# First MLP product of seven column groups by seven block products in place of eight, with the sums of weight blocks on VectorE

## The chip, the core and the metric

The kernel runs on one core of a Trainium2 chip. The core has a matrix engine (TensorE, rows PE for its matmuls and PEld for the loads of its stationary operand), VectorE (DVE), ScalarE (ACT), GpSimd (POOL, unused here) and a queue that issues transfers (SP). They run beside each other and wait for one another by semaphores. The working memory is SBUF; TensorE writes into the banks of PSUM, of which there are eight of 128 x 512 float32. The metric is the device time of one execution in microseconds.

## What is computed

One layer of a hybrid decoder for 256 tokens of width 2048 behind 16 learned tokens: token mixing (gated linear attention and pooling), then a multilayer perceptron (MLP) with 8192 hidden columns, each part added to the residual `h`, and a last norm. All is float32. What matters here:

```python
h = h + mixed @ w_out
z = rmsnorm(h, norm2_w) @ mlp_w1                  # [256, 2048] @ [2048, 8192]
h = h + jnp.square(jax.nn.relu(z)) @ mlp_w2       # [256, 8192] @ [8192, 2048]
return rmsnorm(h, final_norm_w)
```

## The kernel before

**Numbers in two parts.** TensorE runs in a float32 form of reduced precision (`F32R`), so each operand is held as a rounded part `hi` and a rest `lo`, and each product of tiles is three matmuls: hi·hi, hi·lo, lo·hi. The weights come as raw float32 chunks of 128 x 2048 (1 MB), one transfer each (`raw_chunk`, L92, pool `rawp` with 3 buffers), in the order of use. `halves` (L99) splits a chunk into two halves of 128 x 1024: `split` (L74) rounds on ACT (L75, `hi`) and subtracts on DVE (L76, `lo`). The pools `hip` and `lop` have 4 buffers each, so four halves can lie ready or in use.

**The MLP.** The hidden columns are cut into 8 groups of 1024. `mlp1(g)` (L671) makes a group's hidden values: two strips of 512 columns, each from four chunks; `as_chunk` (L208) does one chunk with 24 matmuls of 128 x 512, four k-tiles times the two token tiles times three parts (L217 to L219), into two PSUM banks. The stationary operand is the normed input `u2_hi`, `u2_lo`; the weights stream. At the end of a strip ACT and DVE take relu and square out of PSUM (L683, L685), with the squared 1/rms as the scale, and a deferred step (`back`) turns the result with four transposes per token tile (`turn4`, L635) and splits it (`evac_hl`, L495 to L497) into `z_hi`, `z_lo`. `mlp2(g)` (L697) multiplies them with the group's rows of the second matrix: four strips of two chunks, added to `h` by `add_h` (L627). The loop runs `mlp1(g)`, then `mlp2(g-1)`. The last group's second product stands by itself (L714 to L786), one token tile after the other, with the last norm; its weight `fw` is loaded and scaled early (`load_fw`, `scale_fw`).

**Order.** Deferred steps stand in the list `side`; `run_side` issues one behind each half of a chunk. The framework then puts each engine's instructions into a fixed queue, by the order of the code and by when operands and buffers are expected to be free; each engine works its queue from front to back. `tile_pool(bufs=n)` gives n buffers; a new tile waits until the users of an old one are done.

Of the kernel before, what the change touches and what calls it, by code (L numbers as in the profile page):

```python
# [7 lines left out]
F32 = mybir.dt.float32  # L8
# [3 lines left out]
ALU = mybir.AluOpType  # L12
# [18 lines left out]
# columns of the constants that depend on shapes alone  # L31
# [5 lines left out]
def hybrid_gla_pool_kernel(  # L37
# [35 lines left out]
    # ---------------------------------------------------------------- weights  # L73
# [34 lines left out]
    # -------------------------------------------------------------- constants  # L108
# [14 lines left out]
    # u = rmsnorm(h) without 1/rms, transposed: [channel, token]  # L123
# [21 lines left out]
    # ------------------------------------------------------------- 1 / rms  # L145
# [43 lines left out]
    # --------------------------------------- matrix products, three exact parts  # L189
# [33 lines left out]
    # ================================================================ phase 1  # L223
    # keys: four row blocks at once, in pieces that grow, as the first loads arrive
# [76 lines left out]
    # low-rank gate input, transposed; rows 0..15 and 32..47 add up  # L301
# [14 lines left out]
    # log gates over natural tokens (the factor 1/16 sits in the triangles)  # L316
# [27 lines left out]
    # ke: meta tokens to their end, tile 0 to its end, the first chunk of each tile to its end  # L344
# [43 lines left out]
    # values  # L388
# [24 lines left out]
    # queries  # L413
# [85 lines left out]
    # output gate  # L499
# [38 lines left out]
    # multi-scale pooling  # L538
# [83 lines left out]
    u2_hi = big.tile([P, KD, S], F32R, tag="u_hi", name="u2_hi")  # L622
    u2_lo = big.tile([P, KD, S], F32R, tag="u_lo", name="u2_lo")
# [14 lines left out]
    def make_u2(s, t):  # L638
        ps = turn4(h[:, t, s * 512 : (s + 1) * 512])
        ts = slice(t * P, (t + 1) * P)  # L640
        for j in range(4):
            k = 4 * s + j
            pj = ps[:, j * P : (j + 1) * P]
            act.activation(u2_hi[:, k, ts], pj, AF.Copy, scale=n2[:, k : k + 1])
            dve.scalar_tensor_tensor(
                out=u2_lo[:, k, ts], in0=pj, scalar=n2[:, k : k + 1],
                in1=u2_hi[:, k, ts].bitcast(F32), op0=ALU.mult, op1=ALU.subtract,
            )
# [18 lines left out]
    dve.tensor_tensor(out=rs2, in0=rs2, in1=rs2, op=ALU.mult)  # L667
# [3 lines left out]
    def mlp1(g):  # L671
        nonlocal ci
        z_hi = mp.tile([P, 8, S], F32R, tag="m", name="z_hi")
        z_lo = mp.tile([P, 8, S], F32R, tag="m", name="z_lo")
        rz[g] = (z_hi, z_lo)
        for s in range(2):
            ps = [acc(), acc()]
            for c in range(4):
                as_chunk(ps, ci, u2_hi, u2_lo, 0, 4, 4 * c, c == 0, c == 3)
                ci += 1  # L680
            for t in range(NT):
                r = zt.tile([P, 512], F32, tag="r", name="r")
                act.activation(r, ps[t], AF.Relu, scale=rs2[:, t : t + 1])  # L683
                q = zt.tile([P, 512], F32, tag="q", name="q")
                dve.scalar_tensor_tensor(  # L685
                    out=q, in0=ps[t], scalar=0.0, in1=r, op0=ALU.max, op1=ALU.mult
                )


                def back(s=s, t=t, q=q):  # L690
                    pv = turn4(q).rearrange("p (j c) -> p j c", c=P)
                    ts = slice(t * P, (t + 1) * P)
                    evac_hl(z_hi[:, 4 * s : 4 * s + 4, ts], z_lo[:, 4 * s : 4 * s + 4, ts], pv)

                side.append(back)

    def mlp2(g):  # L697
        nonlocal ci
        z_hi, z_lo = rz.pop(g)
        for s in range(4):  # L700
            ps = [acc(), acc()]
            for c in range(2):
                as_chunk(ps, ci, z_hi, z_lo, 0, 4, 4 * c, c == 0, c == 1)
                ci += 1
            for t in range(NT):
                add_h(ps[t], t, s * 512, (s + 1) * 512)

    mlp1(0)
    side += [load_fw, idle, idle, idle, scale_fw]
    for g in range(1, GROUPS):  # L710
        mlp1(g)
        mlp2(g - 1)
    # ======================================= last group: one token tile after the other
    z_hi, z_lo = rz.pop(GROUPS - 1)  # L714
    e_hi = big.tile([P, KD, S], F32R, tag="u_hi", name="e_hi").rearrange("p k c -> p (k c)")
    e_lo = big.tile([P, KD, S], F32R, tag="u_lo", name="e_lo").rearrange("p k c -> p (k c)")

    def finish(t, w, ps, n):
        # 1/rms out of the sum so far and of the last w columns, still in ps
# [69 lines left out]
def _weights(np, w_in, w_out, w1, w2):  # L789
    """All weights as one run of chunks [128, 2048], in the order in which they are used."""  # L790
    def ws(a):  # [2048, n*256] -> n strips of two chunks, each 8 k-tiles of 256 columns
        n = a.shape[1] // 256
        b = a.reshape(2, 8, P, n, 256).transpose(3, 0, 2, 1, 4)
        return b.reshape(n * 2, P, 2048)

    def st(a):  # [512*c, n*512] -> [n, c] chunks, each 4 k-tiles of 512 columns
# [19 lines left out]
    for g in range(1, GROUPS):  # L816
        m1(g)
# [59 lines left out]
```

## Time and profile before

| | |
|---|---|
| time, median of 3 runs | 1049.33 us (1048.45 to 1050.74) |
| span of the profiled execution | 1046.9 us |
| TensorE matmul busy | 1035.2 us (99%), 5237 matmuls |
| weight load busy | 877.2 us (84%) |
| DVE busy | 605.9 us (58%) |
| ACT busy | 480.6 us (46%) |
| transfers | 197.15 MB, 188 GB/s over the span |

The span is the time from the first to the last instruction; no time of the profiled execution as a whole is given, and the median of the runs is 2.4 us above the span. Matmuls are pipelined and the end of each is modelled, so a matmul's listed time (0.39 us) is longer than the distance to the next one; the distance is the price. Likewise on DVE and ACT a listed time is that of one instruction from its start to its end.

### The profile page before, as it was taken

To read this page: it belongs to the slowest core of one execution; us is meant where nothing else is said; L and a number is where in the kernel's file an instruction comes from. 1 tells how busy PE (TensorE), PEld (TensorE's weight loads), DVE (VectorE), ACT (ScalarE), POOL (GpSimd) and SP (SyncE) were. 2 spreads that over 40 slices of the span, in tenths; PEclk is the share of its full clock that TensorE was granted. 3 is DMA by queue.
4 is the path that set the end of the run, shared out by engine and by line. 5 is a ranking of instruction groups with operands and counts; after the bars stand their busy time and mean duration, and the time that the engine had idled before them with its cause. 6 is when DMAs were issued, how large, how long until landed. Compare 5 with 4: busy or idle time off the path is not lost.

```text
span 1046.9 us, 12935 instructions
## 1 busy us (share of the span) xinstructions
PE 1035.2 (99%) x5237; PEld 877.2 (84%) x5237; DVE 605.9 (58%) x773; ACT 480.6 (46%) x630; POOL 0.2 (0%) x4
## 2 busy tenths in 40 slices
PE   8999999999999999999999999999999999999996
PEld 7989878998888888888888888888888888888885
DVE  7555544876666555555555555565555555555574
ACT  6537544444555444434434433443443344344351
POOL 0000000000000000000000000000000000000000
PEclk9999999999999999999999999999999999999998
DMA  9663434447554545555555555555555555545542
GB/s 348 241 239 137 161 124 159 146 155 288 186 190 172 201 173 189 198 184 182 201 189 179 196 194 184 185 200 186 182 197 191 185 188 199 185 178 201 188 174 81
DMA packets 29820, 197.15 MB, mean 188 GB/s; under 512 B 3456, under 2 KB 3968, under 8 KB 6704
## 3 DMA queue, kind: packets, MB, share of 16 engines
q1 hardware_dynamic: 29760, 196.32, 52.9%
q8 instruction: 41, 0.67, 0.3%
q14 instruction: 19, 0.16, 0.0%
HBM read 194.21 MB, written 2.10 MB: 188 GB/s over the span
## 4 chain that ended last, share of the span: by engine, by line
PE 98%; DMA 1%; SPq 0%; DVE 0%; ACT 0%; issue 0%; ACTq 0%
PE acc L217 25%; PE acc L219 25%; PE acc L218 25%; PE acc L202 4%; PE acc L203 4%; PE acc L204 4%; PE gp L635 2%; PE acc L777 1%; PE acc L776 1%; PE acc L778 1%; DMA raw<-in_wts 1%; PE acc L256 1%; PE acc L258 1%; PE acc L257 1%; PE gp L472 0%; PE gp L473 0%
## 5 line engine op out<-in xcount | busy, mean ns | idle before, releaser
L76 DVE TENSOR_TENSOR lo<-raw,hi 128x1024 fp32r<-128x1024 f32 (+1 forms) x356 | 425.8, 1200 | 373.6 <-ACT hi L75 373.3
L75 ACT CAST hi<-raw 128x1024 fp32r<-128x1024 f32 (+1 forms) x356 | 366.1, 1033 | 484.2 <-PE acc L219 409.4
L217 PE MATMUL acc<-hi,u_hi 128*128 128x512 f32 x576 | 228.5, 397 | 0.0
L219 PE MATMUL acc<-hi,u_lo 128*128 128x512 f32 x576 | 224.8, 390 | 0.0
L218 PE MATMUL acc<-lo,u_hi 128*128 128x512 f32 x576 | 224.5, 390 | 0.0
L217 PE MATMUL acc<-hi,z_hi 128*128 128x512 f32 x448 | 175.7, 392 | 0.0
L219 PE MATMUL acc<-hi,z_lo 128*128 128x512 f32 x448 | 174.5, 389 | 0.0
L218 PE MATMUL acc<-lo,z_hi 128*128 128x512 f32 x448 | 174.4, 389 | 0.0
L219 PEld LDWEIGHTS acc<-hi,u_lo 128*128 128x128 f32 x576 | 108.1, 188 | 23.0
L217 PEld LDWEIGHTS acc<-hi,u_hi 128*128 128x128 f32 x576 | 108.2, 188 | 22.0
L218 PEld LDWEIGHTS acc<-lo,u_hi 128*128 128x128 f32 x576 | 108.3, 188 | 21.7
L219 PEld LDWEIGHTS acc<-hi,z_lo 128*128 128x128 f32 x448 | 84.1, 188 | 17.7
L217 PEld LDWEIGHTS acc<-hi,z_hi 128*128 128x128 f32 x448 | 84.1, 188 | 17.1
L218 PEld LDWEIGHTS acc<-lo,z_hi 128*128 128x128 f32 x448 | 84.2, 188 | 17.0
L202 PE MATMUL acc<-u_hi,hi 128*128 128x272 f32 (+4 forms) x320 | 92.7, 290 | 0.0
L203 PE MATMUL acc<-u_lo,hi 128*128 128x272 f32 (+4 forms) x320 | 91.4, 286 | 0.0
L204 PE MATMUL acc<-u_hi,lo 128*128 128x272 f32 (+4 forms) x320 | 91.2, 285 | 0.0
L202 PEld LDWEIGHTS acc<-u_hi,hi 128*128 128x128 f32 x320 | 60.3, 189 | 1.0 <-issue 0.8
L203 PEld LDWEIGHTS acc<-u_lo,hi 128*128 128x128 f32 x320 | 60.2, 188 | 0.1
L204 PEld LDWEIGHTS acc<-u_hi,lo 128*128 128x128 f32 x320 | 60.1, 188 | 0.0
L627 DVE TENSOR_TENSOR h<-acc,h 128x512 f32<-128x512 f32 (+1 forms) x71 | 45.6, 679 | 5.2 <-PE acc L778 5.2
L683 ACT ACTIVATE r<-acc,rs 128x512 f32<-128x512 f32 x32 | 21.9, 690 | 15.7 <-PE acc L219 15.7
(189 smaller groups left out, 841.6 us busy)
## 6 DMA issues: line engine op xcount, KB each, us to landing
raw<-in_wts SPq DMA_DIRECT2D x175, 1024.0 KB, 4.8
xn<-in_x SPq DMA_DIRECT2D x2, 1024.0 KB, 11.8
h<-in_x SPq DMA_DIRECT2D x2, 1024.0 KB, 6.7
out<-h SPq DMA_DIRECT2D x8, 256.0 KB, 2.9
xTs<-in_xT SPq DMA_DIRECT2D x3, 546.0 KB, 9.7
pw<-in_pool_w SPq DMA_DIRECT2D x4, 256.0 KB, 5.1
fw<-in_rows SPq DMA_DIRECT2D x1, 1024.0 KB, 7.7
raw<-in_wts SPq DMA_DIRECT2D x2, 256.0 KB, 3.5
```

What stands on the lines that cost most here:

```text
L75: act.copy(out=hi, in_=raw)
L76: dve.tensor_tensor(out=lo, in0=raw, in1=hi.bitcast(F32), op=ALU.subtract)
L202: pe.matmul(o, hi[:, cs], u_hi[:, k, lo_t:L], start=k == 0, stop=False)
L203: pe.matmul(o, hi[:, cs], u_lo[:, k, lo_t:L], start=False, stop=False)
L204: pe.matmul(o, lo[:, cs], u_hi[:, k, lo_t:L], start=False, stop=k == KD - 1)
L217: pe.matmul(ps[t], a_hi[:, k, ts], hi[:, cs], start=st, stop=False)
L218: pe.matmul(ps[t], a_hi[:, k, ts], lo[:, cs], start=False, stop=False)
L219: pe.matmul(ps[t], a_lo[:, k, ts], hi[:, cs], start=False, stop=sp)
L256: pe.matmul(o, hi[:, cs], u_hi[:, k, :], start=k == 0, stop=False)
L627: dve.tensor_tensor(out=hs, in0=p, in1=hs, op=ALU.add)
L635: pe.transpose(ps[:, j * P : (j + 1) * P], src[:, j * P : (j + 1) * P], ident)
L683: act.activation(r, ps[t], AF.Relu, scale=rs2[:, t : t + 1])
```

## The change

Groups 1 to 7 no longer call `mlp1`. Their hidden values are a product of [256 x 2048] and [2048 x 1024], seen as 2 x 2 blocks: token tiles times halves of the inner dimension, and these halves times two strips of 512 columns. `group(g)` makes the four blocks of the result from seven block products (`product`, of 128 x 1024 and 1024 x 512) and sums. The seven left operands are made once, in `prepare` (blocks, and sums and differences of blocks, of the input normed with 1/rms), during group 0, which keeps the direct way. The right operands are sums of raw weight blocks, made in place on DVE for each group (`add_raw`, eight additions of 128 x 2048) and split after that like any chunk. The products accumulate in three PSUM banks; `keep` copies three intermediate sums out, and `hidden` adds them where needed and takes relu and square. The eight chunks of the second product of the group before (`half(0)` to `half(7)`) stand between the seven products. The same bytes of weights are loaded, in another order. Pools change: `rawp` 4 buffers, `xy` (4 buffers of 8 KB per partition: first the input's `u2`, then the weight blocks `xs` and `zs`, last the tail's `e`), `zt` 2, and for the MLP 3 + 2 + 3 PSUM banks in place of 4 + 4. `fw` is loaded and scaled behind group 7.

```diff
-    big = ctx.enter_context(tc.tile_pool(name="big", bufs=1))
     mp = ctx.enter_context(tc.tile_pool(name="mp", bufs=4))
-    rawp = ctx.enter_context(tc.tile_pool(name="rawp", bufs=3))
+    rawp = ctx.enter_context(tc.tile_pool(name="rawp", bufs=4))
     hip = ctx.enter_context(tc.tile_pool(name="hip", bufs=4))
     lop = ctx.enter_context(tc.tile_pool(name="lop", bufs=4))
-    accp = ctx.enter_context(tc.tile_pool(name="accp", bufs=4, space=PSUM))
-    gpp = ctx.enter_context(tc.tile_pool(name="gpp", bufs=4, space=PSUM))
-    gt = ctx.enter_context(tc.tile_pool(name="gt", bufs=4))
+    banks = ctx.enter_context(ExitStack())
+    accp = banks.enter_context(tc.tile_pool(name="accp", bufs=4, space=PSUM))
+    gpp = banks.enter_context(tc.tile_pool(name="gpp", bufs=4, space=PSUM))
     gstack = ctx.enter_context(ExitStack())
+    big = gstack.enter_context(tc.tile_pool(name="big", bufs=1))
+    gt = gstack.enter_context(tc.tile_pool(name="gt", bufs=4))
     gq = gstack.enter_context(tc.tile_pool(name="gq", bufs=1))
...
+            gstack.close()
+            xy = ctx.enter_context(tc.tile_pool(name="xy", bufs=4))
+            lp = ctx.enter_context(tc.tile_pool(name="lp", bufs=1))
+            zt = ctx.enter_context(tc.tile_pool(name="zt", bufs=2))
+            gt = gstack.enter_context(tc.tile_pool(name="gt2", bufs=4))
...
-    u2_hi = big.tile([P, KD, S], F32R, tag="u_hi", name="u2_hi")
-    u2_lo = big.tile([P, KD, S], F32R, tag="u_lo", name="u2_lo")
+    u2 = [[xy.tile([P, 8, S], F32R, tag="xy", name="u2") for _ in range(2)] for _ in range(2)]
...
+    while side:
+        side.pop(0)()
+    gstack.close()
+    asp = ctx.enter_context(tc.tile_pool(name="asp", bufs=1))
...
+    def norm_a(kh):
+        a = mp.tile([P, 8, S], F32, tag="m", name="a")
+        full.append(a)
+        u_h, u_l = (u.bitcast(F32) for u in u2[kh])
+        dve.tensor_tensor(out=a, in0=u_h, in1=u_l, op=ALU.add)
+        dve.tensor_tensor(out=a, in0=a, in1=rb2.unsqueeze(1).to_broadcast([P, 8, S]), op=ALU.mult)
...
+    def operand(i, t, kh, sign=1.0):
+        a = blk(t, kh)
+        hi, lo = (asp.tile([P, 8, P], F32R, name=f"{n}{i}") for n in ("ah", "al"))
+        if sign > 0:
+            act.copy(out=hi, in_=a)
+            dve.tensor_tensor(out=lo, in0=a, in1=hi.bitcast(F32), op=ALU.subtract)
+        else:
+            act.activation(hi, a, AF.Copy, scale=-1.0)
+            dve.scalar_tensor_tensor(
+                out=lo, in0=a, scalar=-1.0, in1=hi.bitcast(F32), op0=ALU.mult, op1=ALU.subtract
+            )
+        ops_a[i] = (hi, lo)
...
+        def s5():
+            operand(4, 1, 1)
+            combine((1, 1), (1, 1), (1, 0), ALU.subtract)
+            operand(5, 1, 1)
+        def s7():
+            combine((1, 0), (0, 0), (1, 0), ALU.subtract)
+            operand(7, 1, 0)
+        def s6():
+            combine((0, 0), (0, 0), (1, 1), ALU.add)
+            operand(6, 0, 0, -1.0)
+        def s3():
+            combine((0, 1), (0, 0), (0, 1), ALU.subtract)
+            operand(3, 0, 1)
...
+        return [
+            rms2_rows, lambda: norm_a(0), lambda: operand(1, 0, 0), lambda: norm_a(1),
+            lambda: operand(2, 0, 1), s5, s7, s6, s3,
...
+    banks.close()
+    accp = ctx.enter_context(tc.tile_pool(name="pair", bufs=3, space=PSUM))
+    gpp = ctx.enter_context(tc.tile_pool(name="turn", bufs=2, space=PSUM))
+    sump = ctx.enter_context(tc.tile_pool(name="sum", bufs=1, space=PSUM))
+    def xy_load(c):
+        raw = xy.tile([P, 2048], F32, tag="xy", name="blk")
+        nc.sync.dma_start(out=raw, in_=wts[c])
+        return raw
...
+    def product(i, ps, raws, start):
+        a_hi, a_lo = ops_a[i]
+        for c in range(2):
+            for hf, (hi, lo) in enumerate(halves(raws[c])):
+                for j in range(2):
+                    k = c * 4 + hf * 2 + j
+                    cs = slice(j * 512, (j + 1) * 512)
+                    kw = dict(skip_group_check=True)
+                    pe.matmul(ps, a_hi[:, k], hi[:, cs], start=start and k == 0, stop=False, **kw)
+                    pe.matmul(ps, a_hi[:, k], lo[:, cs], start=False, stop=False, **kw)
+                    pe.matmul(ps, a_lo[:, k], hi[:, cs], start=False, stop=k == 7, **kw)
+            run_side()
...
+    def add_raw(dst, src):
+        dve.tensor_tensor(out=dst, in0=dst, in1=src, op=ALU.add)
+    def keep(ps, name):
+        x = zt.tile([P, 512], F32, tag=name, name=name, bufs=1)
+        act.copy(out=x, in_=ps)
+        return x
+    def hidden(g, s, t, ps, x, sign):
+        q = zt.tile([P, 512], F32, tag="q", name="q")
+        if x is None:
+            r = ps
+        else:
+            r = zt.tile([P, 512], F32, tag="r", name="r")
+            dve.tensor_tensor(out=r, in0=ps, in1=x, op=ALU.add)
+        act.activation(q, r, AF.Relu, scale=sign)
+        act.activation(q, q, AF.Square)
+        side.append(z_back(g, s, t, q))
...
+        def half(j):
+            if j % 2 == 0:
+                pair[:] = [acc(), acc()]
+            as_chunk(pair, base + 8 + j, z_hi, z_lo, 0, 4, 4 * (j % 2), j % 2 == 0, j % 2 == 1)
+            if j % 2:
+                for t in range(NT):
+                    add_h(pair[t], t, j // 2 * 512, (j // 2 + 1) * 512)
+        b_a, b_d, b_b = (sump.tile([P, 512], F32, tag=n, name=n) for n in ("sa", "sd", "sb"))
+        xs = [xy_load(base), xy_load(base + 1)]
+        zs = [xy_load(base + 2), xy_load(base + 3)]
+        product(1, b_a, xs, True)
+        x1 = keep(b_a, "x1")
+        add_raw(xs[0], zs[0])
+        half(0)
+        ys = [raw_chunk(base + 4), raw_chunk(base + 5)]
+        add_raw(xs[1], zs[1])
+        product(5, b_d, xs, True)
+        x5 = keep(b_d, "x5")
+        add_raw(xs[0], ys[0])
+        half(1)
+        add_raw(xs[1], ys[1])
+        product(3, b_d, ys, False)
+        half(2)
+        add_raw(zs[0], ys[0])
+        half(3)
+        add_raw(zs[1], ys[1])
+        product(6, b_a, xs, False)
+        x2 = keep(b_a, "x2")
+        hidden(g, 1, 0, b_d, x2, -1.0)
+        vs = [raw_chunk(base + 6), raw_chunk(base + 7)]
+        add_raw(xs[0], vs[0])
+        half(4)
+        add_raw(xs[1], vs[1])
+        product(7, b_a, zs, False)
+        hidden(g, 1, 1, b_a, x5, -1.0)
+        half(5)
+        product(4, b_a, xs, False)
+        hidden(g, 0, 1, b_a, None, 1.0)
+        half(6)
+        product(2, b_b, vs, True)
+        hidden(g, 0, 0, b_b, x1, 1.0)
+        half(7)
...
+    e = [[xy.tile([P, 2048], F32R, tag="xy", name="e") for _ in range(2)] for _ in range(2)]
+    fw = mp.tile([P, D], F32, tag="m", name="fw")
+    nc.sync.dma_start(out=fw, in_=rows[:, 768 : 768 + D].partition_broadcast(P))
+    dve.tensor_scalar(out=fw, in0=fw, scalar1=-1.0 / 8192.0, scalar2=None, op0=ALU.mult)
...
-        m1(g)
+        for kh, n in ((0, 0), (0, 1), (1, 1), (1, 0)):
+            parts.append(a[2 * g + n, 2 * kh : 2 * kh + 2])
```

## Rows read from the trace of the kernel before

**Rows 1.** The page: busy time by engine; the span in 40 slices.

```profile
PE 1035.2 (99%) x5237; PEld 877.2 (84%) x5237; DVE 605.9 (58%) x773; ACT 480.6 (46%) x630; POOL 0.2 (0%) x4
...
PE   8999999999999999999999999999999999999996
...
DVE  7555544876666555555555555565555555555574
...
PEclk9999999999999999999999999999999999999998
```

**Rows 2.** The chain by engine; then matmuls' waits (line, releaser: us, times, longest).

```profile
PE 98%; DMA 1%; SPq 0%; DVE 0%; ACT 0%; issue 0%; ACTq 0%
...
PE gp L119 <- DVE warm L116: 1.5, 1, 1.5
PE acc L256 <- ACT hi L75: 1.3, 2, 0.7
PE acc L258 <- DVE lo L76: 0.2, 1, 0.2
```

**Rows 3.** Stretches: length, busy us by engine, granted clock, DMA share, GB/s.

```profile
350.50:396.00 45.50, 45.50 (x211) 37.66 (x210) 24.79 (x25) 21.30 (x24) 0.00 (x0) 1.00 0.52 185
484.98:573.95 88.97, 88.97 (x402) 73.65 (x401) 49.13 (x49) 38.19 (x40) 0.00 (x0) 1.00 0.54 189
573.95:662.92 88.97, 88.97 (x403) 73.66 (x401) 49.15 (x49) 38.18 (x40) 0.00 (x0) 1.00 0.53 189
```

**Rows 4.** Timeline of PE, a strip: 19th matmul behind the first; chain, one bank alone.

```profile
477.33 0.39 PE L217 MATMUL acc<-hi,u_hi 128*128 128x512 f32 x1
...
481.41 0.39 PE L217 MATMUL acc<-hi,u_hi 128*128 128x512 f32 x1
...
1030.37 0.23 PE acc L776
...
1031.73 0.23 PE acc L776
```

**Rows 5.** The chain, start us, us: the four transposes of one token tile.

```profile
484.98 0.44 PE gp L635 x4
```

**Rows 6.** DVE and ACT by shape, 485 to 930 us: count, busy, mean ns, idle before.

```profile
L76 DVE TENSOR_TENSOR lo<-raw,hi 128x1024 fp32r<-128x1024 f32 x161 | 197.2, 1225 | 194.9 <-ACT hi L75 194.9
L627 DVE TENSOR_TENSOR h<-acc,h 128x512 f32<-128x512 f32 x40 | 25.6, 682 | 0.0
...
L75 ACT CAST hi<-raw 128x1024 fp32r<-128x1024 f32 x161 | 169.6, 1054 | 245.2 <-PE acc L219 245.2
L683 ACT ACTIVATE r<-acc,rs 128x512 f32<-128x512 f32 x20 | 13.7, 690 | 9.9 <-PE acc L219 9.9
```

**Rows 7.** DVE by shape, whole span: the longest two-operand forms, and `fw`'s scaling.

```profile
L335 DVE SCALAR_TENSOR_TENSOR lg<-g,lg 128x1536 f32<-128x1536 f32 x1 | 1.8, 1759 | 3.3 <-ACT lg L334 3.3
...
L615 DVE TENSOR_SCALAR fw<-fw 128x2048 f32<-128x2048 f32 x1 | 1.2, 1222 | 0.0
```

**Rows 8.** Timeline of DVE: instructions without a gap (merged, xcount), and what follows.

```profile
13.74 2.50 DVE L76 TENSOR_TENSOR lo<-raw,hi 128x512 fp32r<-128x512 f32 x4 [0.84 <-ACT hi L75]
16.16 1.73 DVE L135 SCALAR_TENSOR_TENSOR u_lo<-xTs,u_hi 128x272 fp32r<-128x272 f32 x4
...
32.54 3.49 DVE L76 TENSOR_TENSOR lo<-raw,hi 128x1024 fp32r<-128x1024 f32 x3
```

**Rows 9.** ACT by shape, whole span: the last load of its function table.

```profile
L482 ACT ACT_TABLE_LOAD x1 | 1.3, 1283 | 0.0
```

**Rows 10.** Timeline of ACT and DVE around the end of a strip.

```profile
479.57 1.05 ACT L75 CAST hi<-raw 128x1024 fp32r<-128x1024 f32 x1 [1.67 <-PE acc L219]
481.61 1.37 ACT L683 ACTIVATE r<-acc,rs 128x512 f32<-128x512 f32 x2 [0.99 <-PE acc L219]
482.87 1.04 ACT L75 CAST hi<-raw 128x1024 fp32r<-128x1024 f32 x1
...
480.66 1.23 DVE L76 TENSOR_TENSOR lo<-raw,hi 128x1024 fp32r<-128x1024 f32 x1 [1.50 <-ACT hi L75]
```

**Rows 11.** Issues of transfers: xcount, KB each, us to landing; the queue's own wait.

```profile
raw<-in_wts SPq DMA_DIRECT2D x175, 1024.0 KB, 4.8
...
fw<-in_rows SPq DMA_DIRECT2D x1, 1024.0 KB, 7.7
...
SPq L96 <- DVE lo L76: 848.6, 159, 13.5
```

**Rows 12.** Timeline of DVE in the tail.

```profile
999.81 0.69 DVE L627 TENSOR_TENSOR h<-acc,h 128x512 f32<-128x512 f32 x1 [3.12 <-PE acc L778]
1001.29 0.69 DVE L784 TENSOR_TENSOR h<-h,fw 128x512 f32<-128x512 f32 x1 [0.79 <-ACT junk L630]
```

More of the change, by code (lines that the diff above doesn't have):

```diff
@@ L643, in make_u2 @@
             pj = ps[:, j * P : (j + 1) * P]
-            act.activation(u2_hi[:, k, ts], pj, AF.Copy, scale=n2[:, k : k + 1])
+            u_h, u_l = (u[:, k % 8, ts] for u in u2[k // 8])
+            act.activation(u_h, pj, AF.Copy, scale=n2[:, k : k + 1])
             dve.scalar_tensor_tensor(
-                out=u2_lo[:, k, ts], in0=pj, scalar=n2[:, k : k + 1],
-                in1=u2_hi[:, k, ts].bitcast(F32), op0=ALU.mult, op1=ALU.subtract,
+                out=u_l, in0=pj, scalar=n2[:, k : k + 1], in1=u_h.bitcast(F32), op0=ALU.mult, op1=ALU.subtract,
             )
@@ L697, in mlp2 @@
[L697 to L709, printed above, removed]
+    rs2q = cp.tile([P, NT], F32, name="rs2q")
+    dve.tensor_tensor(out=rs2q, in0=rs2, in1=rs2, op=ALU.mult)
@@ new lines, in hybrid_gla_pool_kernel, with rms2_rows @@
+    rb2 = cp.tile([P, S], F32, name="rb2")
+    while side:
+        side.pop(0)()
+    gstack.close()
+    asp = ctx.enter_context(tc.tile_pool(name="asp", bufs=1))
+    def rms2_rows():
+        ps = gp()
+        for t in range(NT):
+            dg = zt.tile([P, P], F32, tag="q", name="dg2")
+            dve.tensor_scalar(out=dg, in0=ident, scalar1=rs2[:, t : t + 1], scalar2=None, op0=ALU.mult)
+            pe.matmul(ps[:, t * P : (t + 1) * P], cst[:, C_ONE : C_ONE + P], dg, start=True, stop=True)
+        dve.tensor_copy(out=rb2, in_=ps[:, :S])
@@ new lines, in combine, with prepare @@
+    def combine(dst, x0, x1, op):
+        dve.tensor_tensor(out=blk(*dst), in0=blk(*x0), in1=blk(*x1), op=op)
+    def prepare():
+        def s5():
[14 more added lines that the diff above has]
+            lambda: operand(2, 0, 1), s5, s7, s6, s3,
+        ]
@@ new lines, in hybrid_gla_pool_kernel, with z_pair, z_back, back @@
+    rz = {}
+    def z_pair():
+        return [mp.tile([P, 8, S], F32R, tag="m", name=n) for n in ("z_hi", "z_lo")]
+    def z_back(g, s, t, q):
+        def back():
+            z_hi, z_lo = rz[g]
+            pv = turn4(q).rearrange("p (j c) -> p j c", c=P)
+            ts = slice(t * P, (t + 1) * P)
+            evac_hl(z_hi[:, 4 * s : 4 * s + 4, ts], z_lo[:, 4 * s : 4 * s + 4, ts], pv)
+        return back
+    side += [idle] + prepare()
+    rz[0] = z_pair()
+    for s in range(2):
+        ps = [acc(), acc()]
+        for c in range(4):
+            as_chunk(ps, ci, u2[c // 2][0], u2[c // 2][1], 0, 4, 4 * (c % 2), c == 0, c == 3)
+            ci += 1
+        for t in range(NT):
+            r = zt.tile([P, 512], F32, tag="r", name="r")
+            act.activation(r, ps[t], AF.Relu, scale=rs2q[:, t : t + 1])
+            q = zt.tile([P, 512], F32, tag="q", name="q")
+            dve.scalar_tensor_tensor(out=q, in0=ps[t], scalar=0.0, in1=r, op0=ALU.max, op1=ALU.mult)
+            side.insert(t, z_back(0, s, t, q))
@@ new lines, in group @@
+    def group(g):
+        nonlocal ci
+        base = ci
+        ci += 16
+        rz[g] = z_pair()
+        z_hi, z_lo = rz[g - 1]
+        pair = []
+        def half(j):
[3 more added lines that the diff above has]
+            if j % 2:
+                for t in range(NT):
+                    add_h(pair[t], t, j // 2 * 512, (j // 2 + 1) * 512)
[34 more added lines that the diff above has]
+        half(7)
+        del rz[g - 1]
```

47 lines of the change are left out of this document (10 added, 37 removed).

## The prediction, made before the changed kernel ran

> **What bounds the kernel now.** I read the page first: matmuls fill 99% of the span, in every slice but the first and the last, at full granted clock, while DVE stands at 58% and ACT at 46% [rows 1]. The chain that ended last is 98% matmuls, and the matmuls' own waits come to 3 us, all at the start [rows 2]. So in the MLP nothing is late for TensorE, and the time of a group is the count of its matmuls times their distance. The stretches say the same: each group takes 88.97 us, DVE busy for 49.1 of them, ACT for 38.2, clock 1.00 [rows 3]. The distance: 18 matmuls take 4.08 us, 0.2267 each, and six that accumulate in one bank alone take 1.36, the same 0.2267 [rows 4]. Per group 384 x 0.2267 = 87.0, and four turns of 0.44 [rows 5] make 88.8 of the 88.97.
>
> **What is removed.** A direct group's first product is 192 matmuls of 128 x 512, a group with seven products has 7 x 24 = 168 of the same form. The new ones stay in one bank for 24 matmuls, which costs nothing [rows 4]. The second product and the turns stay. So a group may fall to 88.97 - 24 x 0.2267 = 83.5 us, and seven groups give 38.1 us. All of it is on the path, if the other engines keep up.
>
> **What is added on DVE, per group.** Halves to split: 7 x 4 + 8 x 2 = 44 in place of 32. Eight additions of 128 x 2048, for which the trace has no row: 1024 columns take 1.225 [rows 6] and 1536 take 1.759 [rows 7], so 0.534 per 512 and 2.29 for 2048. (The 2048-wide scaling of `fw`, 1.22 [rows 7], has one tensor operand; the lower bound for an addition would be that, but the two-operand rows lie on one line, and I take 2.29.) Fifteen of 512 columns at 0.68 (8 `add_h`, 4 `z_lo`, 3 in `hidden`); the four `q` go to ACT. By listed times: 44 x 1.225 + 8 x 2.29 + 15 x 0.68 = 53.9 + 18.3 + 10.2 = 82.4 us. That is 99% of 83.5, where before it was 55%.
>
> A listed time is not what an instruction costs in a full queue. Four splits listed at 0.686 each are followed by the next instruction after 2.42 us, 0.605 each, and three of 1024 columns end after 3.49, so (3.49 - 1.225) / 2 = 1.13 apart [rows 8]. Starts are some 0.085 closer than the listed times. With 67 instructions the load is 82.4 - 5.7 = 76.7 us, 92% of 83.5. I take this, as the row is of the same instruction; the listed sum is the upper end.
>
> The Trainium skill (VectorE: DVE Perf Modes, section Terms) says that each DVE instruction is followed by a flush, before which the next can't issue. Taken by the letter this speaks against the change, as every instruction would cost its listed time and DVE would carry 82.4 us a group, not 76.7 (the case below in which DVE bounds the head); the overlap speaks against it [rows 8].
>
> **ACT** gets 44 roundings of 1.054, and 3 copies, 4 relus and 4 squares at the 0.69 of L683 [rows 6], and 4 `z_hi`: some 56 of 83.5 us. Enough room. Copy, relu and square alternate in the old kernel too, and the last load of a function table is at L482, ahead of the MLP [rows 9].
>
> **Does the order fit?** Mean load is not enough, because only four halves can lie ready. A half that TensorE frees is rounded in 1.05 and subtracted in 1.23 before the next can use its place. A half of the second product feeds 12 matmuls (2.72 us), one of a product only 6 (1.36). I laid one group out, with DVE at 1.14, 2.21 and 0.60 apart, each engine taking what is ready. The tight place is the head of the group, where four additions fall between the first six units. From the first matmul of product 1 as zero: the first addition ends at -0.7; half 3 of product 1 is split at 0.5, two `add_h` and a `z_lo` follow, half 4 is ready at 3.5 and needed at 4.1. The halves of `half(0)` at 4.6 and 5.7 are needed at 5.4 and 8.2. The second addition runs to 7.9; product 5 has its halves at 9.1, 10.2, 11.4 (needed at 10.9, 12.2, 13.6). Its last half can't be rounded before `half(0)` frees a place at 11.1, so the third addition goes ahead of it, to 13.5, and it is ready at 14.7, needed at 15.0. `half(1)` follows at 15.8 and 17.0 (16.3, 19.0), the fourth addition, and product 3 at 20.3 (21.8). So everything is in time, with 0.3 us to spare at the worst. One addition put in the queue ahead of a split that TensorE is closer to costs 2.2 - 0.3 = 1.9. The queue is fixed beforehand from expected times, so I count one such place in every second group: 1.0 a group, 7 us (bounds 0 and 3.5 a group; the upper one is worked out with the rivals).
>
> **Waits that are added.** `keep` and `hidden` wait on ACT and DVE for the end of a product, and behind them in the queue stand the next roundings. In the old kernel the relu of a strip is the same case: the rounding at 479.57 stands ahead of it, it starts at 481.61, and no matmul waits [rows 2, 10]. I cost these at nothing while four halves lie ahead; one of the rivals prices the loss of that cover. A bank is written again one unit (5.44 us) after it was read, and the reading takes 0.7. The third bank pair waits for two `add_h`, covered by a product (5.44). Turns of the last product come 4 us behind it, under `half(7)`.
>
> **Transfers.** Sixteen chunks a group as before, 189 GB/s [rows 3], 4.7 to 4.8 us to landing; the queue waits for buffers, not for bandwidth [rows 11]. `xs` come free after product 4's splits, three units (16 us) before they are needed: 16 less 4.8 and 2.3 of splitting, 9 to spare.
>
> **Group 0 and its seam.** `prepare` adds to DVE four passes of 2048 (9.2), 11 instructions of 1024 (13.5) and about 1 for the rows of 1/rms: 23.7. Two strips of a first product, which is all of group 0, take 45.5 us with DVE busy for 24.8 [rows 3], so 48.5 listed, 44.9 with the closer starts. Between 0 and 3.0 plus a chunk's two splits, 5.5; I take 2. In group 1 the buffers of `zs` hold `u2` until group 0's last matmul: landing 4.8, addition 2.2, rounding and subtraction 2.3 make 9.3, needed at 10.9; the second is behind it by up to another 4.8, 14.1 against 13.6, with DVE already full. 0 to 5, I take 2. The turns of `u2` are now issued ahead of group 0's first chunk: 0 to 2 (one `add_h` and turn in order), I take 0.5.
>
> **The tail.** `fw` can only be loaded when `z` of group 6 comes free, 7.7 to landing [rows 11] and 1.2 to scale, 8.9. L784 wants it 1.5 after the strip's `add_h` [rows 12], which comes a strip's 24 matmuls (5.44) later, 7. Two us late, with splits behind it on DVE, but up to four halves ahead: 0 to 2, I take 1. The queue issues `fw` in its turn, so chunks behind it could be late too; they wait for the same moment.
>
> **Sum.** 1046.9 - 38.1 + 7 + 2 + 2 + 0.5 + 1 = 1021.3 us of span, and with the 2.4 us by which the median stands above the span 1023.7: **1024 us**. Range of this case 1018 to 1034 (0 to 2 us a group).
>
> **The rivals.**
> - *Clean* (chance 0.20): no addition is ever in the way. 1046.9 - 38.1 + 5.5 + 2.4 = 1017 (1012 to 1018 with the seams at less). For it: the layout has no stall. Against: 0.3 us to spare in a queue that is fixed beforehand.
> - *DVE bounds the head* (0.20): starts come no closer than the listed times. From product 1 to product 3 some 22 instructions are 0.085 later each, 1.9 less the 0.3, so 1.6 a group, and one addition in the wrong place in every group, 1.9: 3.5 x 7 = 24.5 and 1041 (1034 to 1047). Against it: [rows 8]. By the rule of the flush in the Trainium skill (VectorE: DVE Perf Modes, Terms) this case is what comes; the trace so far does not agree with it, with 0.605 from start to start of an instruction listed at 0.686.
> - *The rounding stands behind the product's end* (0.11, slower): ACT's queue keeps the written order, so that after a product ACT first copies (0.69) and then rounds (1.05), DVE subtracts (1.23), and TensorE is dry for these 3.0 and the 0.2 by which a matmul's listed 0.39 outlasts the distance to the next, 3.2 us. It decides at 4.7 us a group (5.44 less the 5.5 of seams over seven), that is from the second such place on; two give 6.4, and 1049.3 + 5.5 + 7 x (6.4 - 5.44) = 1062. Against it: [rows 10].
> - *Nothing left* (0.03): stalls of about 4.7 us a group, 1047 to 1051.
>
> That the change doesn't do what it says I rule out: the count of products is in the code.
>
> **How the numbers follow.** Forecast 0.46, clean 0.20, DVE 0.20, slower 0.11, no change 0.03. Faster by over 0.2% (about what a measurement of this kernel can tell from no change): 0.46 + 0.20 + 0.20 = 0.86. From 1012 to 1046 all but the last two cases lie within; 0.15 is left out.
>
> **What would show it.** Matmuls of the products 168 a group, 0.227 apart; groups of 84 to 85.5 us; DVE busy 80 to 82 of them, by listed times; matmuls of products 1, 5 and 3 waiting for `lo` of L76 behind an addition, and nearly nowhere else. A wait for ACT's rounding right after a product's end would show the slower case; groups of 87 and more, with DVE never idle in the first third, the third one. I am wrong above all if an addition isn't 2.3 us, or if the queue puts additions far ahead of splits.

## The result: 1019.4 us after 1049.95, and the profile after

| | before | after |
|---|---|---|
| median of 4 runs each, us | 1049.95 (1048.45 to 1050.74) | 1019.43 (1019.27 to 1021.5) |
| ratio, 95% interval | | 0.9717 (0.9703 to 0.9731) |
| span of the profiled execution, us | 1046.9 | 1017.7 (own time 1019.51) |
| matmuls | 5237 | 5073 |

Against the forecast of 1024 us the kernel is 4.6 us faster, within the range of the likeliest case (1018 to 1034). But the sum came out near the mark partly because its terms missed in opposite directions.

The page of the kernel after, which answers to [rows 1, 2]: busy time by engine and DVE's row of the slices, then three waits of matmuls and one of weight loads (line, releaser: us, times, longest). L76 and L77 are now the rounding and the subtraction of `split`, L218 to L220 the matmuls of `as_chunk`, L778 to L780 those of `product`, L784 is `add_raw`, L788 the copy in `keep`, L799 the square in `hidden`, L629 the transposes of `turn4`; L257 stands at the start, ahead of the MLP.

```profile
PE 1001.1 (98%) x5073; PEld 843.9 (83%) x5073; DVE 829.4 (81%) x924; ACT 600.6 (59%) x770; POOL 0.2 (0%) x4
...
DVE  7455644776567989979989998997997999899784
...
PE acc L219 <- DVE lo L77: 2.6, 1, 2.6
PE sd L779 <- DVE lo L77: 2.1, 1, 2.1
...
PE acc L257 <- ACT hi L76: 0.9, 2, 0.6
...
PEld gp L629 <- ACT q L799: 6.6, 20, 0.5
```

DVE went from 58 to 81% of the span and from the middle on stands at nine tenths in most slices, and yet in the MLP matmuls wait for it only twice, 2.6 and 2.1 us. Where these two stand is seen in the stretches, here two of the kernel before that the rows ahead of the prediction don't have, group 0 and group 1 (columns as in [rows 3]):

```profile
324.94:370.40 45.46, 45.46 (x210) 37.61 (x209) 27.40 (x44) 22.90 (x33) 0.00 (x0) 1.00 0.53 187
370.40:460.33 89.93, 89.93 (x410) 74.44 (x408) 50.72 (x51) 39.90 (x44) 0.00 (x0) 1.00 0.53 187
```

and of the kernel after group 0, group 1 and group 3, one of six that are alike, which answers to [rows 3]:

```profile
324.70:373.67 48.97, 46.38 (x214) 37.92 (x213) 45.53 (x61) 29.71 (x40) 0.00 (x0) 1.00 0.53 199
373.67:461.87 88.20, 85.74 (x385) 69.61 (x384) 81.23 (x70) 55.75 (x63) 0.00 (x0) 1.00 0.59 217
545.72:629.55 83.83, 83.80 (x377) 68.90 (x376) 78.20 (x68) 54.36 (x59) 0.00 (x0) 1.00 0.55 201
```

The length of group 3 less PE's busy time leaves 0.03 us: with DVE busy for 93% of the group, no matmul waits. Over the whole span, by first matmuls: up to group 0, -0.24 us; group 0, +3.5; group 1, -1.7; groups 2 to 7, 83.85 on average for 88.97, 6 x -5.12 = -30.7; tail and end, -0.1. That is the -29.2 of the span.

DVE and ACT at the head of group 3, against the layout of the prediction. Product 1 begins at 545.72. The shape rows (count, busy, mean ns, idle) stand above the timeline (start, length):

```profile
L784 DVE TENSOR_TENSOR blk<-blk,raw 128x2048 f32<-128x2048 f32 x42 | 96.0, 2287 | 0.2
...
542.49 2.29 DVE L784 TENSOR_TENSOR blk<-blk 128x2048 f32<-128x2048 f32 x1
...
546.52 2.35 DVE L77 TENSOR_TENSOR lo<-blk,hi 128x1024 fp32r<-128x1024 f32 x2
548.79 2.35 DVE L77 TENSOR_TENSOR lo<-raw,hi 128x1024 fp32r<-128x1024 f32 x2
551.06 2.29 DVE L784 TENSOR_TENSOR blk<-blk 128x2048 f32<-128x2048 f32 x1
553.27 3.49 DVE L77 TENSOR_TENSOR lo<-blk,hi 128x1024 fp32r<-128x1024 f32 x3
556.67 2.29 DVE L784 TENSOR_TENSOR blk<-blk,raw 128x2048 f32<-128x2048 f32 x1
558.88 1.22 DVE L77 TENSOR_TENSOR lo<-blk,hi 128x1024 fp32r<-128x1024 f32 x1
```

Counted from 545.72, the three additions end at -0.9, 7.6 and 13.2 us (layout: -0.7, 7.9, 13.5); half 4 of product 1 is ready at 3.15 (3.5); product 5 has its halves at 8.8, 9.9, 11.0 and 14.4 (9.1, 10.2, 11.4, 14.7). The last of them is reached by TensorE at 560.68, that is 15.0. So the estimate of an addition (2.29, row 2.287) and the whole layout held within 0.4 us, and the spare time is 0.6 instead of 0.3.

### The profile page after: what moved, and what is told of

Read it like the earlier page. It is cut to its first block, busy times and chain, and to the rows that moved or that the text cites. A ratio compares the mean times of both kernels' runs of the same rounds, so it can differ in the third digit from the quotient of the medians.

```text
span 1017.7 us, 12947 instructions
## 1 busy us (share of the span) xinstructions
PE 1001.1 (98%) x5073; PEld 843.9 (83%) x5073; DVE 829.4 (81%) x924; ACT 600.6 (59%) x770; POOL 0.2 (0%) x4
## 4 chain that ended last, share of the span: by engine, by line
PE 94%; DVE 4%; DMA 1%; issue 1%; ACT 1%; SPq 0%; ACTq 0%; DVEq 0%
PE acc L219 15%; PE acc L220 15%; PE acc L218 15%; PE sa L779 5%; PE sa L780 5%; PE sa L778 5%; PE acc L203 4%; PE acc L204 4%; PE acc L205 4%; PE sd L779 3%; PE sd L780 2%; PE sd L778 2%; PE gp L629 2%; PE acc L927 1%; PE acc L928 1%; PE acc L926 1%
## 5 line engine op out<-in xcount | busy, mean ns | idle before, releaser
L77 DVE TENSOR_TENSOR lo<-raw,hi 128x1024 fp32r<-128x1024 f32 (+1 forms) x300 | 351.9, 1194 | 115.5 <-ACT hi L76 109.4
L76 ACT CAST hi<-raw 128x1024 fp32r<-128x1024 f32 (+1 forms) x300 | 307.8, 1031 | 211.0 <-PE acc L220 98.5
L76 ACT CAST hi<-blk 128x1024 fp32r<-128x1024 f32 x140 | 147.2, 1054 | 114.6 <-PE acc L220 93.5
L77 DVE TENSOR_TENSOR lo<-blk,hi 128x1024 fp32r<-128x1024 f32 x140 | 166.8, 1221 | 14.4 <-ACT hi L76 12.5
L220 PE MATMUL acc<-hi,z_lo 128*128 128x512 f32 x448 | 175.6, 392 | 0.0
L218 PE MATMUL acc<-hi,z_hi 128*128 128x512 f32 x448 | 174.8, 391 | 0.0
L218 PEld LDWEIGHTS acc<-hi,z_hi 128*128 128x128 f32 x448 | 84.1, 188 | 17.2
L220 PEld LDWEIGHTS acc<-hi,z_lo 128*128 128x128 f32 x448 | 84.2, 188 | 16.9
L784 DVE TENSOR_TENSOR blk<-blk,raw 128x2048 f32<-128x2048 f32 x42 | 96.0, 2287 | 0.2
L780 PE MATMUL sa<-hi,al 128*128 128x512 f32 x224 | 87.3, 390 | 0.0
L779 PE MATMUL sa<-lo,ah 128*128 128x512 f32 x224 | 87.2, 390 | 0.0
L778 PE MATMUL sa<-hi,ah 128*128 128x512 f32 x224 | 87.2, 389 | 0.0
L779 PEld LDWEIGHTS sa<-lo,ah 128*128 128x128 f32 x224 | 42.0, 188 | 8.8
```

Of the source, the lines that this page charges most:

```text
L76: act.copy(out=hi, in_=raw)
L77: dve.tensor_tensor(out=lo, in0=raw, in1=hi.bitcast(F32), op=ALU.subtract)
L218: pe.matmul(ps[t], a_hi[:, k, ts], hi[:, cs], start=st, stop=False)
L220: pe.matmul(ps[t], a_lo[:, k, ts], hi[:, cs], start=False, stop=sp)
L778: pe.matmul(ps, a_hi[:, k], hi[:, cs], start=start and k == 0, stop=False, **kw)
L779: pe.matmul(ps, a_hi[:, k], lo[:, cs], start=False, stop=False, **kw)
```

## The experiments

Each is an edit to the kernel after. `issue_after(x)` puts what stands inside it behind `x` in its engine's queue.

**One addition behind another.** In group 1 of the kernel after, DVE's queue has the addition for product 7 (`zs[0] += ys[0]`) ahead of the one for product 5 (`xs[1] += zs[1]`). The edit puts it behind:

```diff
-        add_raw(xs[1], zs[1])
+        second = add_raw(xs[1], zs[1]).ins
...
-        add_raw(zs[0], ys[0])
+        with tc.issue_after(second):
+            add_raw(zs[0], ys[0])
```

> One edge of order added to the changed kernel: on DVE the addition zs[0] += ys[0] may not stand ahead of xs[1] += zs[1]. In the changed kernel group 1 has it ahead, and product 5 then waits 2.1 us for a split at 388 us of the span; the steady groups have it behind already. Theory, a misplaced addition: the wait goes, group 1 falls from 88.2 us by about 2.2 to 86.0, the steady groups stay at 83.85, the time falls from 1019.4 to about 1017. Rival, the late landing of the zs chunks is the cause (their buffers hold u2 until 373.4 us and they land 6 to 7 us after their issue): the second zs lands at about 381 and the first half of product 5 waits as before, group 1 stays at 88, the time at 1019.

DVE's timeline in group 1, first of the kernel after, then of this one; the same stretch of 86.33 us closes the second:

```profile
382.34 2.28 DVE L784 TENSOR_TENSOR blk<-blk,raw 128x2048 f32<-128x2048 f32 x1
384.54 2.29 DVE L784 TENSOR_TENSOR blk<-blk 128x2048 f32<-128x2048 f32 x1
386.74 4.63 DVE L77 TENSOR_TENSOR lo<-blk,hi 128x1024 fp32r<-128x1024 f32 x4
...
388.02 0.50 PE L779 MATMUL sd<-lo,ah 128*128 128x512 f32 x1 [2.11 <-DVE lo L77]
```

```profile
382.34 2.28 DVE L784 TENSOR_TENSOR blk<-blk 128x2048 f32<-128x2048 f32 x1
384.54 4.62 DVE L77 TENSOR_TENSOR lo<-blk,hi 128x1024 fp32r<-128x1024 f32 x4
...
373.66:459.99 86.33, 85.79 (x385) 69.61 (x384) 80.65 (x70) 55.92 (x63) 0.00 (x0) 1.00 0.59 222
```

The operands tell the two additions apart: `blk,raw` adds a chunk of `ys`, `blk` one of `zs`. With the order changed the splits start 2.2 us earlier, the wait is gone, and group 1 takes 1.87 us less. The time is 1018.44 us (1017.5 to 1019.71), ratio 0.9713 (0.9696 to 0.9729); this interval overlaps that of the kernel after, so it is the length of group 1 that tells the two apart. The addition for product 5 now starts at 382.34 without a pause, so its blocks were there in time, and the late landing falls as the cause of the wait. This is the one misplaced addition of the kernel. Its net price is near the 1.9 of the prediction, in part by luck: the wait that goes is 2.1 us, and at 419 some 0.5 us is lost that the kernel after doesn't lose there, at a first matmul of product 7 that waits for a copy (the account below has a case of this kind).

**`prepare` in single steps.** The nine steps, of up to three DVE instructions each, are cut into 16, one behind each half from the start of group 0 on, and their order changes a little (`sum_a` and `scale_a` are the two passes of `norm_a`):

```diff
-            rms2_rows, lambda: norm_a(0), lambda: operand(1, 0, 0), lambda: norm_a(1),
-            lambda: operand(2, 0, 1), s5, s7, s6, s3,
+            rms2_rows, lambda: sum_a(0), lambda: scale_a(0), lambda: operand(1, 0, 0),
+            lambda: sum_a(1), lambda: scale_a(1), lambda: operand(4, 1, 1),
+            lambda: combine((1, 1), (1, 1), (1, 0), ALU.subtract), lambda: operand(5, 1, 1),
+            lambda: operand(2, 0, 1),
+            lambda: combine((1, 0), (0, 0), (1, 0), ALU.subtract), lambda: operand(7, 1, 0),
...
-    side += [idle] + prepare()
+    side += prepare()
```

> The changed kernel with the preparation of the left operands in 16 single steps, one behind each half of a chunk, in place of 9 larger ones; the last two fall into group 1. Theory, a queue of DVE work placed ahead of a split: DVE is busy 45.5 of the 49.0 us of group 0 and the wait of 2.6 us at 355 us comes from two combinations and two subtractions standing ahead of one split; spread out it goes, group 0 falls from 49.0 us to 46 to 47, the time to about 1017. Rival, the load itself: what is taken out of group 0 comes back as a wait in group 1, where DVE works without a pause until 400 us; groups 0 and 1 together stay at 137 us and the time at 1019.

What it had to move, in DVE's timeline of the kernel after: the split that TensorE waits for at 354.94 stands behind six instructions of `prepare` (two of L705, two of L696) and of the strip's end (two of L757).

```profile
347.86 1.22 DVE L705 TENSOR_TENSOR a<-a 128x1024 f32<-128x1024 f32 x1
...
350.73 0.69 DVE L757 SCALAR_TENSOR_TENSOR q<-acc,r 128x512 f32<-128x512 f32 x1
351.39 2.36 DVE L696 TENSOR_TENSOR al<-a,ah 128x1024 fp32r<-128x1024 f32 x2
353.66 1.22 DVE L77 TENSOR_TENSOR lo<-raw,hi 128x1024 fp32r<-128x1024 f32 x1
354.94 0.50 PE L219 MATMUL acc<-lo,u 128*128 128x512 f32 x1 [2.58 <-DVE lo L77]
```

In single steps, groups 0 and 1, and the longest wait that is left in them:

```profile
324.72:370.82 46.10, 46.10 (x213) 37.89 (x212) 43.91 (x60) 29.17 (x40) 0.00 (x0) 1.00 0.58 216
370.82:458.02 87.20, 85.93 (x385) 69.45 (x384) 81.98 (x72) 55.78 (x63) 0.00 (x0) 1.00 0.58 217
...
PE sd L770 <- DVE lo L77: 0.8, 1, 0.8
```

Group 0 takes 46.10 for 48.97 and PE is busy for all of it, with 60 instructions on DVE in that stretch for 61 (43.91 us busy for 45.53): the price was the clump, not the load. 1016.26 us (1015.7 to 1016.92), ratio 0.9688 (0.9674 to 0.9702).

**Both edits together.** Groups 0 and 1:

> Both edits together. If the two waits are two misplaced pieces of work they add up: groups 0 and 1 together fall from 137.2 us by 4 to 5, the time from 1019.4 to about 1015. If DVE's load over groups 0 and 1 bounds them (126.8 us busy, against 130 us of matmuls at their distance), they give at most half of it, and the time is 1017 or more.

```profile
325.32:371.47 46.15, 46.15 (x214) 37.90 (x212) 43.91 (x60) 29.18 (x40) 0.00 (x0) 1.00 0.57 216
371.47:458.65 87.18, 85.89 (x385) 69.47 (x384) 81.97 (x72) 55.90 (x63) 0.00 (x0) 1.00 0.59 217
```

1015.94 us (1015.41 to 1016.33), ratio 0.9684 (0.967 to 0.9699): faster than the kernel after, by intervals that don't overlap, but not to be told apart from the version before it (1016.26). The edits don't add up. With `prepare` spread, group 1 is entered in another state and its queue is laid out anew, so that of the 2.1 us wait only 0.8 was left, and the fixed order does not take that (0.8 stays). Both groups together gain 3.8 of 7.0 us, a bit less than the 4 to 5 that I expected. Group 1 still takes 2.5 us more than 84.7, which would be a steady group and two turns of group 0. In its trace 1.0 of them stands at the wait of 0.8, and 0.8 and 0.5 at 390 and 418, where the first matmuls of products 3 and 7 wait for a copy of `keep`. Why the 0.8 us wait for `lo` is left wasn't followed further.

**Without the sums of weight blocks.**

```diff
     def add_raw(dst, src):
-        dve.tensor_tensor(out=dst, in0=dst, in1=src, op=ALU.add)
+        pass
```

> The changed kernel without the eight sums of weight blocks of each group: DVE loses 56 instructions of 2.29 us, 128 us in all; the hidden values of groups 1 to 7 are then those of unsummed blocks. Theory, the sums are hidden but for one place in group 1: the steady groups stay at 83.5 to 83.85 us, only the 2.3 us of group 1 go, the time is about 1016 to 1017. Rival, the additions cost something in each group (the 0.3 us by which a group is longer than its matmuls and turns are priced): the steady groups fall to 83.4, and the time to 1014. Second rival, contention for the memory between DVE and the weight stream: the distance of the matmuls, 0.2267 us, falls.

```profile
376.28:461.49 85.21, 85.12 (x385) 69.69 (x384) 64.19 (x62) 55.90 (x63) 0.00 (x0) 1.00 0.61 225
545.71:629.93 84.22, 84.13 (x377) 68.91 (x376) 62.71 (x60) 54.27 (x59) 0.00 (x0) 1.00 0.55 200
...
PE acc L257 <- ACT hi L76: 2.1, 3, 1.2
PEld gp L629 <- ACT q L799: 9.5, 21, 0.5
```

1020.68 us (1019.39 to 1021.31), ratio 0.9728 (0.9714 to 0.9743): no faster, against what I expected (1016 to 1017). Group 1 loses its wait, as it should. But a group in which DVE is busy for 62.7 instead of 78.2 us takes 84.22, not less than 83.85. Three of its four turns, in place of one, now wait 0.19 us for the square on ACT, 9.5 us of waits of weight loads for 6.6. And ahead of anything that this edit touches, L257 waits 1.2 us longer, and between 60 and 100 us the granted clock is 0.96 for 1.00; group 0 begins 2.6 us later (327.34 for 324.70). So the time says little here, and the groups decide: in a group the eight sums cost TensorE nothing, and the expectation had failed to see that other queues move when one gets shorter. Nor do they slow the matmuls: without them the 24 of a product still take 5.44 us (583.79 to 589.23).

**The same work in two places.** An addition's twin (a maximum of a block with itself, which leaves it as it is) once behind the first addition, at the head of the group; or twice behind product 4, in its last third:

```diff
         add_raw(xs[0], zs[0])
+        dve.tensor_tensor(out=xs[0], in0=xs[0], in1=xs[0], op=ALU.max)
```

> The changed kernel with one more DVE instruction of 128 x 2048 in each group, at its head: xs[0] is written onto itself (its maximum with itself) between the first addition and the splits of product 5. DVE is busy 78.2 of 83.85 us of a steady group, so by the mean load 2.2 us more still fit. Theory, the place decides: at the head DVE works without a pause for some 58 us and is in time by 0.3 us at the worst, so a group grows by about 1.9, to 85.7, and the time from 1019.4 to about 1033. Rival, mean load: it fits, 83.85 and 1019. Second rival, the listed times are the price (82.4 us a group before, 84.7 with it): 84.9 and 1026.

```diff
         product(4, b_a, xs, False)
+        dve.tensor_tensor(out=xs[0], in0=xs[0], in1=xs[0], op=ALU.max)
+        dve.tensor_tensor(out=xs[1], in0=xs[1], in1=xs[1], op=ALU.max)
```

> The changed kernel with two more DVE instructions of 128 x 2048 in each group, at its end: xs[0] and xs[1] are written onto themselves behind product 4, where DVE pauses. Theory, starts 0.085 us closer than the listed times and the place decides: 78.2 + 4.4 = 82.6 of 83.85 us, all in the pauses, no group grows by more than 0.3 us, the time stays at 1019 to 1021. Rival, the listed times are the price: 82.4 + 4.6 = 87.0 us of DVE in a group, 3.2 more than it lasts, the time is about 1041.

A steady group with one at the head, and a wait of it; then one with two in the last third:

```profile
548.80:634.48 85.68, 84.69 (x377) 68.83 (x376) 80.17 (x69) 54.41 (x59) 0.00 (x0) 1.00 0.53 197
...
555.36 0.50 PE L219 MATMUL acc<-lo,z_hi 128*128 128x512 f32 x1 [0.50 <-DVE lo L77]
...
566.80 0.50 PE L778 MATMUL sd<-hi,ah 128*128 128x512 f32 x1 [0.23 <-ACT x L788]
```

```profile
549.15:633.05 83.90, 83.83 (x377) 68.92 (x376) 82.08 (x70) 54.30 (x59) 0.00 (x0) 1.00 0.55 201
```

At the head 2.2 us of DVE cost 1.85 us a group (1031.87 us, one run, beside 1049.2 of the kernel before); in the last third 4.4 us cost 0.05, with DVE busy for 82.08 of 83.90. So it is the place that decides. The 1.85 is the size that 2.2 less the layout's 0.3 of cover gives, but that is luck, as it isn't one wait for `lo`. Some 0.8 us is lost there (0.50 listed as wait; the matmul starts 0.89 behind the one before it, in place of 0.23). Twice 0.5 is lost where TensorE's queue has the first matmul of product 3 or of product 7 among those of the half ahead of it, and that matmul waits for `keep` to copy its bank (0.23 listed as wait). In group 3 of the kernel after they stand behind the half. Why the queue was laid out anew isn't shown. The second kernel's time, 1023.15 us (one run), is 3.7 above the kernel after for a reason outside the steady groups; it stands under the hardware, below.

**Three places for halves in place of four.**

```diff
-    hip = ctx.enter_context(tc.tile_pool(name="hip", bufs=4))
-    lop = ctx.enter_context(tc.tile_pool(name="lop", bufs=4))
+    hip = ctx.enter_context(tc.tile_pool(name="hip", bufs=3))
+    lop = ctx.enter_context(tc.tile_pool(name="lop", bufs=3))
```

> The changed kernel with three buffers for the rounded halves and three for the rests in place of four each (hip and lop). The load is the same, only the lead is shorter by one half. Theory, the lead covers the additions: within a product a half lasts 1.36 us, a place that comes free is filled 2.3 us later and only two halves (2.7 us) are ahead, so each of the four additions at the head (2.2 us) and those before products 6, 7 and 4 make TensorE wait, 1 to 2 us each: groups of 90 to 96 us, the gain of the change is gone, 1060 to 1100 us. Rival, a lead of three is as good: 83.85 us a group, 1019.

```profile
560.30:649.94 89.64, 85.81 (x377) 68.31 (x376) 78.28 (x68) 54.35 (x59) 0.00 (x0) 1.00 0.51 188
```

DVE does the same work (78.28 us for 78.20) and the group takes 5.8 us more, a bit under the 90 that I expected at the least. Over the span, matmuls of L218 wait 11.8 us for `hi` of L76 and those of L779 5.0 us for `lo` of L77, where the kernel after has one wait of 2.1 on these. The time is 1068.73 us (one run), slower than the kernel before: with three places the gain is gone. The kernel before was not run with three, so what it would lose itself isn't known.

**Copies ahead of the next roundings.** The slower rival, made by hand: on ACT, the three copies of `keep` stand ahead of the roundings of the unit that follows.

```diff
     def keep(ps, name):
-        act.copy(out=x, in_=ps)
-        return x
+        return x, act.copy(out=x, in_=ps).ins
...
-        x1 = keep(b_a, "x1")
+        x1, k1 = keep(b_a, "x1")
...
+        with tc.issue_after(k1):
+            half(0)
...
+        with tc.issue_after(k5):
+            half(1)
...
+        with tc.issue_after(k2):
+            half(4)
```

> The changed kernel with three edges of order on ACT: the copies that keep the sums of products 1, 5 and 6 stand ahead of the roundings of the unit that follows, as the code has them written; in the changed kernel the queue has three roundings ahead of the copy. Theory, the slower rival of the prediction: after each of the three products TensorE is dry for the copy, one rounding and one subtraction, 0.5 + 1.05 + 1.23 and 0.2 to the release, 2.9 us, so 8.8 us a group: 92.6 us, slower than before by some 30 us, about 1080. Rival, halves that are split ahead cover it: under 1 us a place, below 87 us a group and 1040.

ACT behind product 5, and a group:

```profile
488.94 0.59 ACT L788 COPY x<-sd 128x512 f32<-128x512 f32 x1 [4.16 <-PE sd L780]
489.42 3.89 ACT L76 CAST hi<-raw 128x1024 fp32r<-128x1024 f32 x4
...
469.05:561.86 92.81, 85.67 (x377) 68.53 (x376) 79.49 (x68) 53.19 (x59) 0.00 (x0) 1.00 0.49 181
561.86:657.81 95.95, 88.81 (x377) 70.76 (x376) 79.68 (x68) 53.16 (x59) 0.00 (x0) 0.96 0.47 176
...
PE acc L218 <- ACT hi L76: 34.1, 21, 1.7
```

ACT idles for 4.2 us with the copy at its front, then copies and rounds four halves in a row. A group at full clock takes 92.81, 9.0 more, on average 3.0 for each of three places, where the rival had 3.2. The next group is another 3.1 longer, at a granted clock of 0.96. 1091.31 us (one run): with this order in ACT's queue the change would have lost 4% to the kernel before. In the kernel after the same queue has a rounding (547.28) ahead of the copy (551.36), as in [rows 10].

## Why the prediction was right, and where it was not

**Right: what bounds it, and the saving.** 24 matmuls fewer a group, all on the path. The distance in one bank held: product 1 begins at 545.72, `half(0)` at 551.16, 24 x 0.2267. The saving was 5.12 us and not 5.44, so 35.8 for 38.1. The missing 0.3 lies in the turns: 360 x 0.2267 + 4 x 0.44 = 83.4, and 83.85 were measured. The turn of the last product comes close behind its square, and its weight load waits for ACT:

```profile
626.12 0.39 PE L218 MATMUL acc<-hi,z_hi 128*128 128x512 f32 x1
626.54 0.66 PE L629 MATMUL gp<-cst,q 128*128 128x128 f32 x4
```

0.42 from start to start in place of 0.23. This is 0.19 of the 0.3, the rest is spread over the turns. I had written that this turn comes 4 us behind its product, and so in time; it comes 3.1 us behind it (the half begins at 623.40), and I had not followed its chain of sum, relu and square.

**Right: the load of DVE.** Closer starts than listed times were the step on which most hung. Splits of two follow each other after 2.27 us in the head shown above, 1.135 each for 1.22 listed, and the twins show the limit: a group with ten passes of 2048 would by listed times need 82.4 + 2 x 2.29 = 87.0 us of DVE, and was done in 83.90. The Trainium skill (VectorE: DVE Perf Modes, section Terms) has each instruction wait for the flush of the one before it; by that rule, taken by the letter, this group would have taken 87 us, and the trace does not agree. The formula for a float32 addition in the Trainium skill (VectorE: DVE Perf Modes, section The TRN2 errata) gives an estimate of 2.29 us for 2048 columns; the row agrees with 2.287. The case of DVE bounding the head, at 1041, falls with it.

**Wrong: the misplaced additions.** "One such place in every second group", 7 us, was the step that made the forecast differ from the clean case. In groups 2 to 7 there is none; there is one in group 1, and it is the only place where matmuls of products 1, 5 and 3 wait for `lo`, the sign that I had named. The price came out near (1.87 net by the first experiment, 1.9 in the text), the number of places was a guess, and no row of the kernel before bore on it. The queue met the layout with its few tenths to spare in all six groups alike. Within the groups it is the clean case that came. Why the planner misplaced the one in group 1 isn't shown: its expected times are not in the trace.

**Too small: the seams.** 4.5 us were predicted (2 for `prepare`, 0.5 for the turns of `u2`, 2 for group 1); 3.5 + 3.5 were measured, the second against 83.85 and the two turns of group 0 that fall into group 1 (0.88), 84.7. In group 0 the sum counted the load against 45.5 us of time (between 0 and 5.5). It took DVE's 24.8 us from a stretch that begins in the middle of group 0 (350.50 to 396.00); group 0 itself has 27.4, as its row above shows. Even so the load alone did cost little: 46.10 when spread. What it left out is that a clump of six instructions ahead of a split costs 2.6 whatever the mean load. In group 1 I named late blocks of `zs`, at 2 us; it was 3.5, and of another cause. The misplaced addition of the first experiment makes 2.4 of it (two matmuls start 2.50 apart, the next 0.34 behind, in place of 0.23 each). Another 0.8 stands at the end of product 5, in TensorE's own queue:

```profile
393.37 0.61 PE L218 MATMUL acc<-hi,z_hi 128*128 128x512 f32 x2
394.20 0.50 PE L778 MATMUL sd<-hi,ah 128*128 128x512 f32 x1 [0.22 <-ACT x L788]
...
395.10 0.40 PE L220 MATMUL acc<-hi,z_lo 128*128 128x512 f32 x1
```

The first matmul of product 3 (L778) stands between those of `half(1)`, ahead of the copy of its bank by `keep`, and four matmuls take 1.73 us in place of 0.91. So `keep`, which the sum had at nothing, cost 0.8 in group 1, and nothing in group 3, where product 3 follows behind `half(1)`.

**The tail** cost 0.05 us, not 1: `fw` landed in 4.4 us, not 7.7 [rows 11], and was scaled by 971.0, 3.2 ahead of the first instruction that wants it at 974.25. **Around the span** lie 1.8 us (1019.51 less 1017.7), not the 2.4 taken from the median.

The sum with measured terms: 1046.9 - 35.8 + 0 + 7.0 + 0 - 0.4 (up to group 0, and the end) = 1017.7, with the misplaced addition of group 1 among the 7.0 of the seams. Too high by 7 and 1 and too low by 2.5 and 2.3: the errors cancelled by more than half, and that is luck.

**The slower rival** was rightly seen and priced: 3.0 a place, and two places (6.0) would have outweighed 5.12. It did not come since ACT's queue has the roundings first, as [rows 10] showed.

## What to carry to other kernels

Exchanging matmuls for vector additions pays as long as the vector engine stays short of full, even at 93% and more, when its work is laid out against the times at which TensorE needs it: 2.2 us of it cost 1.85 at the group's head and next to nothing in its last third. Price an addition by its place and by how many prepared operands lie ahead of TensorE, not by the share of busy time, and look for clumps where one-off work meets the stream, and in TensorE's queue for a matmul that stands ahead of the copy of its bank. Before predicting waits from a queue that a planner lays out, find a row that shows how it orders such cases; without one, count the places as unknown and say so.

## Of the hardware: the clock after a wait

The wait of 2.6 us in group 0 stands in the kernel after and in the one with two twins alike. Six microseconds around it (columns as in [rows 3]), first after, then with the twins, with matmuls behind the wait:

```profile
354.00:360.00 6.00, 5.06 (x22) 4.21 (x23) 6.00 (x7) 1.75 (x3) 0.00 (x0) 1.00 0.62 191
```

```profile
354.00:360.00 6.00, 4.71 (x14) 3.78 (x15) 6.00 (x8) 1.74 (x3) 0.00 (x0) 0.74 0.57 186
...
355.29 0.50 PE L219 MATMUL acc<-lo,u 128*128 128x512 f32 x1 [2.59 <-DVE lo L77]
...
357.16 0.63 PE L218 MATMUL acc<-hi,u 128*128 128x512 f32 x1
357.59 0.63 PE L219 MATMUL acc<-lo,u 128*128 128x512 f32 x1
```

After the same idle time the granted clock stayed at 1.00 in the one, and fell in the other: 0.74 over the six microseconds, with matmuls 0.43 apart in place of 0.23 behind the wait, about twice as far, as at the lower of the two levels (1.2 and 2.4 GHz). Group 0 took 50.60 us there for 48.97, so such a wait can cost 1.6 us more than its length. In group 1 the same happened between 390 and 400 (clock 0.83), and that group took 89.59 for 88.20: 3.0 of the 3.7 us by which that run is longer. Why the clock fell in the one run and not in the other, no run here shows.
